# First norm's weights as the scale of the operations that split the turned tokens, with engine orders fixed around them

## The chip, the cores and the metric

The kernel runs on one core of one Trainium2 chip. The metric is the device time of one execution in microseconds. The engines are named as the profile names them: PE (TensorE, its weight loads as PEld), DVE (VectorE), ACT (ScalarE), POOL (GpSimd) and SP (SyncE, which issues the DMAs). A number such as L265 is a line of the kernel.

## The reference

One block of a streaming encoder: 16 learned meta tokens are put ahead of 512 tokens of width 1024. Two branches read one normalised input, a stick-breaking attention (8 heads) and a gated linear attention (GLA, 4 heads); they are merged by sigmoid gates, and a gated feed-forward stage with a causal convolution follows. The change touches the first norm and the first projections:

```python
h = jnp.concatenate([meta, x], axis=1)          # 528 tokens x 1024
hn = _rmsnorm(h, norm_mix_pre[l])               # x * rsqrt(mean(x^2) + eps) * g
proj = hn @ w_in[l]                             # all projections of both branches
g_q, g_k, g_v, g_r, g_lr = ...                  # slices of proj
glog = log_sigmoid(g_lr @ w_gk_up[l] + b_gk[l]) / 16
...
```

## The kernel before

Activations are held by feature: 128 features on the partitions, tokens along the free dimension, eight feature groups `k`. Every product has float32 accuracy by splitting both factors into a rounded high piece and a low remainder; a projection is three products for each `k` (high by high, low x by high w, high x by low w). A weight is loaded raw by SP, cast by ACT to its high piece (L90) and subtracted to its low piece (L91) on DVE or POOL.

The start of the program, with which the change deals, goes like this. Four token tiles of 128 (`xt1` to `xt4`) and the meta tokens (`xm`, as 128 rows of 128) are loaded with tokens on the partitions. For each, ACT sums the squares (L247) and a short chain of one-column operations gives 1/rms (L120 to L132); DVE scales the identity with it (L213, `drin`, two buffers). PE multiplies the tile by that diagonal (L265, `tp`): this turns it to features on the partitions and applies 1/rms in one. A 128 by 128 float32 product is two passes on PE, so a turn of one tile is 16 passes, in two PSUM tiles of 512 columns (four pieces `k` each). `split_g` then multiplies by the norm's weights (DVE, L206, `yg`, 128x512), casts the high piece (ACT, L207, `hnh`) and subtracts the low one (DVE or POOL, L208, `hnl`). The norm's weights `gT` come from an 8x128 load that PE turns (L234). Warming products (L230), whose result nobody reads, stand ahead of the first turn (10 of them) and behind turn 0, that of the meta tokens (6).

The first projections are k and q of GLA head 0 (L111, `pt_gk`, `pt_gq`), each in two halves of tokens: columns 0 to 271 (meta tokens, tiles 1 and 2) and 272 to 527 (tiles 3 and 4). With them come the gate's rank product (L383, `lr`), its copies (`gst`, L384 to L387), the gate products (L390, `pg`) with the weights `wg` (L372, L373), and then the v projections (`pt_gv`). Eight transposes of small tables (L305, L308: convolution weights, other norms' weights, the last two meta tokens) stand among the rank products; six DMAs load what they turn.

The order on each engine is made by a scheduler that places instructions by its own estimate of their times; `tc.issue_after(i)` pins what is built under it behind instruction `i`. A tile pool with `bufs=2` makes the third tile of a tag wait for the readers of the first. An instruction waits for others only through counters, one for each engine and DMA queue.

Of the kernel before, what the change touches and what calls it, by code (L numbers as in the profile page):

```python
# [16 lines left out]
P = 128  # L17
D = 1024
# [33 lines left out]
def block_kernel(ctx: ExitStack, tc: tile.TileContext, x, meta_tokens, norm_mix_pre, w_in, w_gk_up, b_gk,  # L52
# [26 lines left out]
    last_raw = [None]  # L79

    def load_w(src, nk, name, hi_out=None, lo_out=None, lo_eng=pool, into=None):
# [8 lines left out]
        act.copy(hi_out, raw)  # L90
        lo_eng.tensor_tensor(out=lo_out, in0=raw, in1=f32(hi_out), op=ALU.subtract)  # L91
        return hi_out, lo_out
# [7 lines left out]
    def proj(w, xh, xl, segs, name, apart=False):  # L100
# [4 lines left out]
        pt = mmt(f"pt_{name}")  # L105
        segs = [(pt[:m, 512 - l1 + l0 : 512], l0, l1), (pt[:m, 512 : 512 + l2 - l1], l1, l2)]
        steps = [(k, a, b) for k in range(nk) for a, b in ((wh, xh), (wh, xl), (wl, xh))]
        for grp in ([[s] for s in segs] if apart else [segs]):
            for n, (k, a, b) in enumerate(steps):
                for dst, lo, hi in grp:  # L110
                    pe.matmul(dst, a[:, k, :], b[:, k, lo:hi], start=n == 0, stop=n == len(steps) - 1)  # L111
        return pt[:m, 512 - l1 + l0 : 512 + l2 - l1]
# [56 lines left out]
    tables(SET_LN_EXP)  # L169
    ident = cst.tile([P, P], F32, name="ident")  # L170
    make_identity(nc, ident)
    p00 = ExitStack()
    p0c = p00.enter_context(tc.tile_pool(name="p0c", bufs=1, side="right"))
# [3 lines left out]
    tmpc = p0c.tile([P, P], F32, name="tmpc")  # L177
    pool.memset(tmpc, -1.0)
    pool.tensor_copy(neg1, tmpc)

    pool.affine_select(out=tmpc, in_=tmpc, compare_op=ALU.is_ge, fill=0.0, base=0, pattern=[[-1, P]], channel_multiplier=1)
    pool.tensor_copy(tri, tmpc)
    pool.memset(ucum, 1.0 / 16.0)
    pool.affine_select(out=ucum, in_=ucum, compare_op=ALU.is_ge, fill=0.0, base=0, pattern=[[1, P]], channel_multiplier=-1)

    ghT = cst.tile([P, 2], F32, name="ghT")
    cw = cst.tile([P, 4, FT], F32, name="cw")
# [21 lines left out]

    def diagonal(pl, r, n, nm):  # L210

        d = pl.tile([P, P], F32, tag="dr", name=f"dr{nm}", bufs=2)
        dve.tensor_scalar(out=d[:n, :n], in0=ident[:n, :n], scalar1=r, scalar2=None, op0=ALU.mult)  # L213
        return d[:n, :n]

    with tc.tile_pool(name="p0", bufs=2, side="right") as p0:
# [3 lines left out]
        g8 = p0.tile([KT, P], F32, name="g8", bufs=1)  # L220
        for i in (1, 2):
            sp.dma_start(xts[i], x[(i - 1) * P : i * P, :])
        sp.dma_start(g8, norm_mix_pre[0].rearrange("(k p) -> k p", p=P))
        sp.dma_start(xm, meta_tokens.rearrange("t (k p) -> (t k) p", p=P))

        def warm(n, nm):

            tp = pst(f"warm{nm}", "z")
            for _ in range(n):
                pe.matmul(tp[:, :P], ident, ident, start=True, stop=True)  # L230
# [11 lines left out]
        def stats(i, after=None):  # L242
            xt = xts.get(i, xm)
            junk = p0.tile([P, D], F32, tag="junk", name=f"junk{i}", bufs=1)
            ss = p0.tile([P, 1], F32, tag="ss", name=f"ss{i}")
            with tc.issue_after(after.ins) if after else ExitStack():
                act.activation(junk[:, : xt.shape[1]], xt, AF.Square, accum_out=ss)  # L247
            if not i:
                tp = pst("ssm")
                pe.matmul(tp[:, :1], same, ss, start=True, stop=True)  # L250
                ss = tp[:, :1]
            return diagonal(p0, rstd_of(p0, ss, D, f"in{i}"), P, f"in{i}")

        def turned(i, dr):
            if not i:
                tp = pst("tpm")
                last_tp[0] = pe.matmul(tp[:, :P], xm, dr, start=True, stop=True)
                split_g(p0, hnh[:, :, :NM], hnl[:, :, :NM], tp[:, :P].rearrange("p (t k) -> p k t", k=KT), gT, "m")
                return
            t = slice(NM + (i - 1) * P, NM + i * P)  # L260
            for b in range(2):
                tp = pst(f"tp{i}_{b}", "sz"[i % 2])
                for k in range(4):
                    c = (4 * b + k) * P
                    last_tp[0] = pe.matmul(tp[:, k * P : (k + 1) * P], xts[i][:, c : c + P], dr, start=True, stop=True)  # L265
                ks = slice(4 * b, 4 * b + 4)
                low = split_g(p0, hnh[:, ks, t], hnl[:, ks, t], tp.rearrange("p (k t) -> p k t", k=4), gT[:, ks], f"{i}_{b}", LO[i][b])
            return low

        last_tp = [None]  # L270
        LO = {1: (pool, pool), 2: (dve, pool), 3: (dve, pool), 4: (dve, pool)}
        d1 = stats(1)
        d2 = stats(2, last_exp[0])
        turned(1, d1)
        d0 = stats(0, last_exp[0])
        low2 = turned(2, d2)
        with tc.issue_after(last_exp[0].ins), tc.issue_after(last_yg[0].ins):
# [15 lines left out]
        cr = p0.tile([FT, 4, P], F32, name="cr", bufs=1)  # L293
        sp.dma_start(cr[:, 0:3, :], conv_w.rearrange("r (m p) -> m r p", p=P))
        sp.dma_start(cr[:, 3, :], conv_b[0].rearrange("(m p) -> m p", p=P))
        small = []
        for t, src in ((ghT, gla_head_norm[0]), (g1T, norm_mix_post[0]), (g2T, norm_ffn_pre[0]), (mT, meta_tokens[T0:, :])):
            n = src.shape[0] // P if len(src.shape) == 1 else src.shape[0] * KT
            r = p0.tile([n, P], F32, name=f"small{len(small)}", bufs=1)
            sp.dma_start(r, src.rearrange("(k p) -> k p" if len(src.shape) == 1 else "t (k p) -> (t k) p", p=P))  # L300
            small.append((t, r, n))
        with tc.issue_after(last_tp[0].ins):
            tp = pst("cwt")
            for r in range(4):
                pe.transpose(tp[:, r * FT : (r + 1) * FT], cr[:, r, :], ident[:FT, :FT])  # L305
            o = 4 * FT
            for t, r, n in small:
                pe.transpose(tp[:, o : o + n], r, ident[:n, :n])  # L308
                o += n
        act.copy(cw, tp[:, : 4 * FT].rearrange("p (r m) -> p r m", r=4))  # L310
        o = 4 * FT
        for t, r, n in small:
            src = tp[:, o : o + n]
            dve.tensor_copy(t, src.rearrange("p (t k) -> p t k", k=KT) if t is mT else src)
            o += n

    p00.close()
# [859 lines left out]
```

## Time and profile before

| | us |
|---|---|
| median of 3 runs | 955.11 (954.68 to 955.27) |
| profiled execution | 956.72 |
| its span, first to last instruction | 954.8 |

The mean granted clock of the span is 0.990. A row of the timeline gives start, length, engine, line, operation, output and inputs, form, count, and in brackets the idle time ahead of it with what ended it. A row of the chain gives start, length and what it was. Rows with x16 or x32 join neighbours of one kind; a matmul's own length overlaps the next one's, so its pace is read from starts. Times in the text are from the span's start.

### The profile page before, as it was taken

The page shows a single profiled execution, that of the slowest core. Times are in us where ns is not written, and L with a number is a line of the kernel's source. Part 1 is how long each engine was busy: PE and PEld are TensorE (multiplying, and loading weights), DVE is VectorE, ACT ScalarE, POOL GpSimd, SP SyncE. Part 2 cuts the span into 40 slices and gives each one's busy share as a digit, 9 for nine tenths or more (in the row PEclk, how much of TensorE's full clock was granted, in tenths as well). Part 3 has the DMA queues.
Part 4 walks back from the last instruction along what each step waited for, and adds up shares of the span by engine and source line. Part 5 has one row for each costly group of instructions (what it writes and reads, how often), then busy time and mean ns, then how long its engine had stood idle before and what let it go on. Part 6 is the DMA issues. An engine that isn't in the chain of part 4 may idle for free.

```text
span 954.8 us, 17806 instructions
## 1 busy us (share of the span) xinstructions
PE 926.2 (97%) x7164; PEld 854.3 (89%) x7164; DVE 655.4 (69%) x1110; ACT 492.3 (52%) x933; POOL 360.7 (38%) x262
## 2 busy tenths in 40 slices
PE   7999999999999998999999899999999999999996
PEld 7999999999999997999998679999999999988785
DVE  5676858687558785888849957554555444578987
ACT  5664656555467674676663245433333333255654
POOL 5433242333355444554445443544444444100200
PEclk9999999999999999999999999999999999999999
DMA  7122222212223212231214453333333333274923
GB/s 209 55 68 67 69 67 67 68 50 78 63 60 87 65 49 66 67 90 47 77 56 113 145 184 111 90 89 99 100 89 89 90 104 93 90 253 159 254 94 121
DMA packets 129731, 92.85 MB, mean 97 GB/s; under 512 B 4064, under 2 KB 114914, under 8 KB 129650
## 3 DMA queue, kind: packets, MB, share of 16 engines
q1 hardware_dynamic: 126178, 82.55, 29.4%
q0 software_dynamic: 1504, 2.88, 1.8%
q10 hardware_dynamic: 1968, 6.29, 1.8%
q8 instruction: 56, 0.92, 0.4%
q14 instruction: 25, 0.20, 0.1%
HBM read 87.52 MB, written 4.19 MB: 96 GB/s over the span
## 4 chain that ended last, share of the span: by engine, by line
PE 82%; DVE 10%; issue 3%; ACT 3%; POOL 2%; DMA 1%; DVEq 0%; ACTq 0%; POOLq 0%
PE pt_up L111 13%; PE ga L963 13%; PE pt_gv L111 5%; PE pt_gr L111 5%; PE pt_go L111 4%; PE pt_mg L111 4%; PE dA L1025 3%; PE dD L1025 3%; PE pt_gk L111 3%; PE pt_sv L111 2%; PE pt_gq L111 2%; PE dB L1025 2%; PE pt_ms L111 2%; PE wo L897 2%; PE pt_sk L111 2%
## 5 line engine op out<-in xcount | busy, mean ns | idle before, releaser
L91 POOL TENSOR_TENSOR wl_up<-raw_up,wh_up 128x1024 fp32r<-128x1024 f32 x22 | 53.0, 2410 | 67.9 <-ACT wh_up L90 67.9
L91 POOL TENSOR_TENSOR wl_ga<-raw_ga,wh_ga 128x1024 fp32r<-128x1024 f32 x22 | 55.2, 2510 | 56.6 <-ACT wh_ga L90 56.6
L111 PE MATMUL pt_up<-h2l,wh_up 128*128 128x256 f32 (+1 forms) x352 | 73.7, 283 | 0.5 <-POOL h2l L208 0.2
L111 PE MATMUL pt_up<-h2h,wh_up 128*128 128x256 f32 (+1 forms) x352 | 73.6, 283 | 0.2
L111 PE MATMUL pt_up<-h2h,wl_up 128*128 128x256 f32 (+1 forms) x352 | 73.2, 282 | 0.0
L963 PE MATMUL ga<-h2l,wh_ga 128*128 128x512 f32 (+1 forms) x192 | 72.2, 376 | 0.0
L963 PE MATMUL ga<-h2h,wl_ga 128*128 128x512 f32 (+1 forms) x192 | 72.2, 376 | 0.0
L963 PE MATMUL ga<-h2h,wh_ga 128*128 128x512 f32 (+1 forms) x192 | 72.0, 375 | 0.0
L90 ACT CAST wh_up<-raw_up 128x1024 fp32r<-128x1024 f32 x22 | 23.0, 1049 | 85.3 <-PE pt_up L111 76.2
L111 PEld LDWEIGHTS pt_up<-h2h,wh_up 128*128 128x128 f32 x352 | 56.9, 189 | 2.2 <-ACT h2h L207 0.5
L111 PEld LDWEIGHTS pt_up<-h2l,wh_up 128*128 128x128 f32 x352 | 55.5, 189 | 1.1 <-DVE h2l L208 0.7
L111 PEld LDWEIGHTS pt_up<-h2h,wl_up 128*128 128x128 f32 x352 | 55.4, 189 | 0.0
L963 PEld LDWEIGHTS ga<-h2h,wl_ga 128*128 128x128 f32 x192 | 36.2, 189 | 7.0
L954 DVE SCALAR_TENSOR_TENSOR cy<-pt_up,cw,cy 128x511 f32<-128x511 f32 (+1 forms) x22 | 16.4, 745 | 37.7 <-ACT cy L951 37.7
L963 PEld LDWEIGHTS ga<-h2l,wh_ga 128*128 128x128 f32 x192 | 36.1, 188 | 6.2
L963 PEld LDWEIGHTS ga<-h2h,wh_ga 128*128 128x128 f32 x192 | 36.2, 188 | 6.1
L954 DVE SCALAR_TENSOR_TENSOR yp<-pt_up,cw,yp 128x511 f32<-128x511 f32 (+1 forms) x22 | 16.4, 745 | 30.9 <-ACT yp L951 30.9
L90 ACT CAST wh_ga<-raw_ga 128x1024 fp32r<-128x1024 f32 x22 | 23.0, 1048 | 25.2 <-PE ga L963 24.7
L1053 POOL DMA_DIRECT2D tv<-in_w_ffn_down_dram x6 | 7.1, 1178 | 68.0 <-DVE wl_p L139 68.0
L91 POOL TENSOR_TENSOR wl_gr<-raw_gr,wh_gr 128x1024 fp32r<-128x1024 f32 x8 | 19.1, 2386 | 36.0 <-ACT wh_gr L90 27.1
L138 ACT CAST sh_p<-As 128x512 fp32r<-128x512 f32 (+1 forms) x30 | 17.4, 584 | 28.9 <-PE dB L1025 12.1
L111 PE MATMUL pt_gr<-hnh,wh_gr 128*128 128x258 f32 (+1 forms) x128 | 28.2, 294 | 0.0
(555 smaller groups left out, 3222.6 us busy)
## 6 DMA issues: line engine op xcount, KB each, us to landing
raw_up<-in_w_ffn_up_dram SPq DMA_DIRECT2D x22, 512.0 KB, 3.8
raw_ga<-in_w_ffn_gate_dram SPq DMA_DIRECT2D x22, 512.0 KB, 3.9
raw_t<-in_w_ffn_down_dram SPq DMA_DIRECT2D x10, 512.0 KB, 7.5
raw_gv<-in_w_in_dram SPq DMA_DIRECT2D x8, 512.0 KB, 3.8
raw_gr<-in_w_in_dram SPq DMA_DIRECT2D x8, 512.0 KB, 3.9
raw_mg<-in_w_in_dram SPq DMA_DIRECT2D x8, 512.0 KB, 3.9
raw_go<-in_w_gla_out_dram SPq DMA_DIRECT2D x8, 512.0 KB, 4.2
raw_ms<-in_w_in_dram SPq DMA_DIRECT2D x8, 512.0 KB, 3.9
```

The costliest lines, as they stand in the source:

```text
L90: act.copy(hi_out, raw)
L91: lo_eng.tensor_tensor(out=lo_out, in0=raw, in1=f32(hi_out), op=ALU.subtract)
L111: pe.matmul(dst, a[:, k, :], b[:, k, lo:hi], start=n == 0, stop=n == len(steps) - 1)
L138: act.copy(hi, src)
L897: pe.matmul(d0[i], m[k][:, t], w, start=k == 0 and q == 0, stop=k == 7 and q == 2)
L954: dve.scalar_tensor_tensor(out=y[:, d:], in0=pt[:, : SEQ - d], scalar=c, in1=y[:, d:], op0=ALU.mult, op1=ALU.add)
L963: pe.matmul(pg_[:, lo:hi], a[:, k, :], b[:, k, lo:hi], start=lo == 0 and k == 0 and q == 0, stop=k == KT - 1 and q == 2, skip_group_check= ...
L1025: mm[i] = pe.matmul(dsts[i], a, b, start=first and k == 0 and j == 0, stop=last and k == NP - 1 and j == 2, skip_group_check=True)
L1053: return lambda n, q, nk: pool.dma_start(out=t[:, q : q + nk, :], in_=block(s, c, q, nk), accum_op=ALU.add)
```

## The change

A new input `by_feature` (128x130, float32) holds the first norm's weights, three other small tables, two meta tokens and the convolution weights and biases, already with features on the partitions; the host only reshapes and joins them. One DMA loads it, and the transposes, their copies and their loads go. For the token tiles, `split_g` is replaced by operations on pieces of 128 columns that read PSUM directly: ACT writes the high piece as `tp` times `gT`, DVE writes the low piece as `tp` times `gT` minus the high piece. `split_g` stays for the meta tokens. The meta tokens' squares go to DVE, and their diagonal is made before that of tile 2. Three warming products stand ahead of turn 1, none behind turn 0. The low piece of q's weights moves from POOL to DVE. Tiles 3 and 4 are turned after the first halves of both k and q, and POOL builds masks and triangles later.

```diff
+        sp.dma_start(xts[1], x[0:P, :])
         sp.dma_start(xm, meta_tokens.rearrange("t (k p) -> (t k) p", p=P))
+        sp.dma_start(xts[2], x[P : 2 * P, :])
+        sp.dma_start(bf, by_feature)
...
         warm(10, 0)
-        tp = pst("g")
-        pe.transpose(tp[:, :KT], g8, ident[:KT, :KT])
-        act.copy(gT, tp[:, :KT])
...
+                sqm = p0.tile([P, P], F32, name="sqm", bufs=1)
+                dve.tensor_tensor(out=sqm, in0=xm, in1=xm, op=ALU.mult)
+                dve.tensor_reduce(out=ss, in_=sqm, op=ALU.add, axis=mybir.AxisListType.X)
...
-                ks = slice(4 * b, 4 * b + 4)
-                low = split_g(p0, hnh[:, ks, t], hnl[:, ks, t], tp.rearrange("p (k t) -> p k t", k=4), gT[:, ks], f"{i}_{b}", LO[i][b])
+                for k in range(4 * b, 4 * b + 4):
+                    c = slice((k - 4 * b) * P, (k - 4 * b + 1) * P)
+                    with tc.issue_after(last_hi[0].ins) if last_hi[0] else ExitStack():
+                        last_hi[0] = act.mul(hnh[:, k, t], tp[:, c], gT[:, k : k + 1])
+                    with tc.issue_after(last_yg[0].ins) if last_yg[0] else ExitStack():
+                        last_yg[0] = dve.scalar_tensor_tensor(out=hnl[:, k, t], in0=tp[:, c], scalar=gT[:, k : k + 1],
+                                                              in1=f32(hnh[:, k, t]), op0=ALU.mult, op1=ALU.subtract)
...
         d1 = stats(1)
+        d0 = stats(0, last_exp[0])
+        with tc.issue_after(last_tp[0].ins):
+            warm(3, 1)
         d2 = stats(2, last_exp[0])
...
-            first["q"] = load_w(cols(w_in, C_GQ), KT, "gq0")
-        turned(3, d3)
-        low4 = turned(4, d4)
+            first["q"] = load_w(cols(w_in, C_GQ), KT, "gq0", lo_eng=dve)
...
+        begun = {nm: proj(first[nm], hnh, hnl, ALL, f"g{nm}0", apart=True, only=(0,)) for nm in "kq"}
+        with tc.issue_after(last_pr[0].ins):
+            turned(3, d3)
+            turned(4, d4)
...
-            for r in range(4):
-                pe.transpose(tp[:, r * FT : (r + 1) * FT], cr[:, r, :], ident[:FT, :FT])
...
-                w = first[nm] if h == 0 else load_w(cols(w_in, c0), KT, f"g{nm}{h}")
-                pt = proj(w, hnh, hnl, ALL, f"g{nm}{h}", apart=h == 0)
+                if h == 0:
+                    with tc.issue_after(after_lr[0].ins):
+                        pt = proj(first[nm], hnh, hnl, ALL, f"g{nm}{h}", apart=True, only=(1,), pt=begun[nm])
```

In the rows below, `tp_0` and `tp_1` are the two PSUM tiles of a turn, numbers at the end of a name count buffers, and brackets name the counters that an instruction waits for (an engine's, or a DMA queue's as DMAHW). First PE before, from the first instruction to the first product of k:

```order
L230 MATMUL warm_112<-ident 128x128 x9
L234 MATMUL g<-ident,g_107 128x8 [waits DMAHW2_49]
L265 MATMUL tp_0_156<-drin_141,xt_102 128x128 [waits DMAHW0_49,DVE_49]
L250 MATMUL ssm<-ss_175,same 128x1 [waits Activation_49,Pool_49]
L265 MATMUL tp_0_189<-drin_154,xt_103 128x128 [waits DMAHW1_49,DVE_49]
L257 MATMUL tpm<-drin_187,xm 128x128 [waits DMAHW3_49,DVE_49,PE_49]
L230 MATMUL warm_221<-ident 128x128 x6
L111 MATMUL pt_gk_483<-hnh,wh_gk_209 128x272 [waits Activation_49]
L111 MATMUL pt_gk_483<-hnl,wh_gk_209 128x272 [waits DVE_49,Pool_49]
L111 MATMUL pt_gk_483<-hnh,wl_gk_210 128x272
L111 MATMUL pt_gk_483<-hnh,wh_gk_209 128x272
L111 MATMUL pt_gk_483<-hnl,wh_gk_209 128x272
```

And the same stretch of PE in the changed kernel:

```order
L225 MATMUL warm_96<-ident 128x128 x9
L246 MATMUL ssm<-ss_124,same 128x1 [waits DVE_49,Pool_49]
L225 MATMUL warm_140<-ident 128x128 x3
L262 MATMUL tp_0_157<-drin_122,xt_86 128x128 [waits DMAHW0_49,DVE_49,PE_49]
L254 MATMUL tpm<-drin_138,xm 128x128 [waits DMAHW1_49,DVE_49]
L262 MATMUL tp_0_195<-drin_155,xt_87 128x128 [waits DMAHW2_49,DVE_49]
L262 MATMUL tp_1_208<-drin_155,xt_87 128x128 [waits DVE_49]
L115 MATMUL pt_gk_255<-hnh,wh_gk_185 128x272 [waits Activation_49]
L115 MATMUL pt_gk_255<-hnl,wh_gk_185 128x272 [waits DVE_49]
L115 MATMUL pt_gk_255<-hnh,wl_gk_186 128x272
L115 MATMUL pt_gk_255<-hnh,wh_gk_185 128x272 [waits Activation_49]
L115 MATMUL pt_gk_255<-hnl,wh_gk_185 128x272 [waits DVE_49]
```

The turn of the meta tokens moved ahead of tile 2's, warming products ahead of turn 1, and the products of k wait for ACT and DVE at each piece, not once.

On ACT before, from the first split to the casts of the second tile:

```order
L207 CAST hnh<-yg_0_161 128x4x128 [waits DVE_49]
L207 CAST hnh<-yg_1_170 128x4x128 [waits DVE_49]
L90 CAST wh_gk_209<-raw_gk_207 128x1024 [waits DMAHW4_49]
L247 ACTIVATE junk_228,ss_229<-xt_104 128x1024 [waits DMAHW5_49]
L207 CAST hnh<-yg_0_194 128x4x128 [waits DVE_49]
L207 CAST hnh<-yg_1_203 128x4x128 [waits DVE_49]
```

And in the changed kernel, up to the cast of q's weights:

```order
L266 ACTIVATE hnh<-tp_0_157,bf 128x128 [waits DMAHW3_49,PE_49]
L266 ACTIVATE hnh<-tp_0_157,bf 128x128 [waits DVE_49] x3
L266 ACTIVATE hnh<-tp_1_170,bf 128x128 [waits PE_49]
L266 ACTIVATE hnh<-tp_1_170,bf 128x128 [waits DVE_49] x3
L90 CAST wh_gk_185<-raw_gk_183 128x1024 [waits DMAHW4_49]
L198 CAST hnh<-ygm 128x8x16 [waits DVE_49]
L266 ACTIVATE hnh<-tp_0_195,bf 128x128 [waits PE_49]
L266 ACTIVATE hnh<-tp_0_195,bf 128x128 [waits DVE_49] x3
L90 CAST wh_gq_225<-raw_gq_223 128x1024 [waits DMAHW7_49]
```

Two casts a tile became eight multiplies, and six of the eight wait for DVE; the weights' casts stand behind a whole token tile.

DVE of the changed kernel in the same stretch:

```order
L206 TENSOR_SCALAR drin_155<-ident,a_in_152 128x128 [waits DVE_49,PE_49]
L268 SCALAR_TENSOR_TENSOR hnl<-tp_0_157,bf,hnh 128x128 [waits DMAHW3_49,Activation_49]
L268 SCALAR_TENSOR_TENSOR hnl<-tp_0_157,bf,hnh 128x128 [waits Activation_49] x3
L268 SCALAR_TENSOR_TENSOR hnl<-tp_1_170,bf,hnh 128x128 [waits Activation_49] x4
L197 TENSOR_TENSOR ygm<-tpm,bf 128x128 [waits PE_49]
L91 TENSOR_TENSOR wl_gk_186<-raw_gk_183,wh_gk_185 128x1024 [waits DMAHW4_49,Activation_49]
L268 SCALAR_TENSOR_TENSOR hnl<-tp_0_195,bf,hnh 128x128 [waits Activation_49] x4
L91 TENSOR_TENSOR wl_gq_226<-raw_gq_223,wh_gq_225 128x1024 [waits DMAHW7_49,Activation_49]
```

Each low piece waits for ACT; the diagonal of tile 2 (`drin_155`) now stands ahead of the lows of tile 1 and waits for PE, and the low piece of q's weights stands behind those of tile 2.

More of the change, by code (lines that the diff above doesn't have):

```diff
@@ L98, in wrows, with proj @@
         return w[k0 * P : (k0 + nk) * P, c0:c1].rearrange("(k p) m -> p k m", p=P)
-    def proj(w, xh, xl, segs, name, apart=False):
+    last_pr = [None]
+    def proj(w, xh, xl, segs, name, apart=False, only=None, pt=None):
         wh, wl = w
@@ L104, in proj @@
         (l0, l1), (_, l2) = segs
-        pt = mmt(f"pt_{name}")
+        begins = only and pt is None
+        pt = mmt(f"pt_{name}") if pt is None else pt
         segs = [(pt[:m, 512 - l1 + l0 : 512], l0, l1), (pt[:m, 512 : 512 + l2 - l1], l1, l2)]
         steps = [(k, a, b) for k in range(nk) for a, b in ((wh, xh), (wh, xl), (wl, xh))]
+        segs = [segs[i] for i in only] if only else segs
         for grp in ([[s] for s in segs] if apart else [segs]):
@@ L176, in block_kernel @@
     ucum = cst.tile([P, P], F32, name="ucum")
[L177 to L187, printed above, removed]
+    bf = cst.tile([P, sum(WIDTHS)], F32, name="bf")
+    gT, ghT, g1T, g2T, mT, cw = (bf[:, sum(WIDTHS[:i]) : sum(WIDTHS[: i + 1])] for i in range(len(WIDTHS)))
+    mT = mT.rearrange("p (t k) -> p t k", k=KT)
+    cw = cw.rearrange("p (r m) -> p r m", m=FT)
     p1 = ExitStack()
@@ L219, in block_kernel @@
         xm = p0.tile([P, P], F32, name="xm", bufs=1)
[L220 to L223, printed above, removed]
+        sp.dma_start(xts[1], x[0:P, :])
         sp.dma_start(xm, meta_tokens.rearrange("t (k p) -> (t k) p", p=P))
+        sp.dma_start(xts[2], x[P : 2 * P, :])
+        sp.dma_start(bf, by_feature)
+        tables(SET_LN_EXP)
+        last_tp = [None]
         def warm(n, nm):
@@ L229, in warm @@
             for _ in range(n):
[L230 removed]
+                last_tp[0] = pe.matmul(tp[:, :P], ident, ident, start=True, stop=True)
         warm(10, 0)
[L233 to L235 removed]
         same = p0.tile([P, P], F32, name="same", bufs=1)
@@ L242, in stats @@
         def stats(i, after=None):
-            xt = xts.get(i, xm)
-            junk = p0.tile([P, D], F32, tag="junk", name=f"junk{i}", bufs=1)
             ss = p0.tile([P, 1], F32, tag="ss", name=f"ss{i}")
-            with tc.issue_after(after.ins) if after else ExitStack():
[L247 to L252, printed above, removed]
+            if i:
+                junk = p0.tile([P, D], F32, tag="junk", name=f"junk{i}", bufs=1)
+                with tc.issue_after(after.ins) if after else ExitStack():
+                    act.activation(junk, xts[i], AF.Square, accum_out=ss)
+            else:
+                sqm = p0.tile([P, P], F32, name="sqm", bufs=1)
+                dve.tensor_tensor(out=sqm, in0=xm, in1=xm, op=ALU.mult)
+                dve.tensor_reduce(out=ss, in_=sqm, op=ALU.add, axis=mybir.AxisListType.X)
+                tp = pst("ssm")
+                with tc.issue_after(last_tp[0].ins):
+                    last_tp[0] = pe.matmul(tp[:, :1], same, ss, start=True, stop=True)
+                ss = tp[:, :1]
+            with tc.issue_after(after.ins) if after else ExitStack():
+                return diagonal(p0, rstd_of(p0, ss, D, f"in{i}"), P, f"in{i}")
         def turned(i, dr):
@@ new lines, in turned @@
+                for k in range(4 * b, 4 * b + 4):
+                    c = slice((k - 4 * b) * P, (k - 4 * b + 1) * P)
+                    with tc.issue_after(last_hi[0].ins) if last_hi[0] else ExitStack():
[3 more added lines that the diff above has]
+                                                              in1=f32(hnh[:, k, t]), op0=ALU.mult, op1=ALU.subtract)
@@ L296, in block_kernel @@
[L296 to L303, printed above, removed]
-            for r in range(4):
[L305 to L317, printed above, removed]
+        first_half = last_hi[0], last_yg[0]
+        with tc.issue_after(first_half[0].ins), tc.issue_after(first_half[1].ins):
+            first["q"] = load_w(cols(w_in, C_GQ), KT, "gq0", lo_eng=dve)
+            d3 = stats(3)
+            d4 = stats(4)
@@ new lines, in block_kernel @@
+        with tc.issue_after(wst_lo.ins):
+            tmpc = pgc.tile([P, P], F32, name="tmpc")
+            pool.memset(tmpc, -1.0)
+            pool.tensor_copy(neg1, tmpc)
+            pool.affine_select(out=tmpc, in_=tmpc, compare_op=ALU.is_ge, fill=0.0, base=0, pattern=[[-1, P]], channel_multiplier=1)
+            pool.tensor_copy(tri, tmpc)
+            pool.memset(ucum, 1.0 / 16.0)
+            pool.affine_select(out=ucum, in_=ucum, compare_op=ALU.is_ge, fill=0.0, base=0, pattern=[[1, P]], channel_multiplier=-1)
```

155 lines of the change are left out of this document (75 added, 80 removed).

## The prediction

> **What bounds the kernel now.** First the summary of busy time and the chain of work that ended last.
>
> ```profile
> PE 926.2 (97%) x7164; PEld 854.3 (89%) x7164; DVE 655.4 (69%) x1110; ACT 492.3 (52%) x933; POOL 360.7 (38%) x262
> ...
> PE 82%; DVE 10%; issue 3%; ACT 3%; POOL 2%; DMA 1%; DVEq 0%; ACTq 0%; POOLq 0%
> ```
>
> TensorE is busy for 97% of the span, and DMA holds only 1% of the chain. So nothing later in the program absorbs a delay: a microsecond that PE loses at the start is a microsecond at the end. The diff reaches only the first 45 us (and the order of a few rows near 570 us), so I read the busy time by stretches of the start, then the chain there.
>
> ```profile
> 0.00:13.00 13.00, 10.61 (x55) 10.29 (x55) 4.13 (x14) 7.10 (x17) 7.00 (x26) 1.00 0.86 256
> 13.00:25.00 12.00, 9.61 (x78) 9.08 (x77) 11.14 (x21) 7.21 (x17) 5.77 (x5) 1.00 0.65 158
> 25.00:40.00 15.00, 15.00 (x123) 14.26 (x122) 11.77 (x26) 10.06 (x20) 5.72 (x11) 1.00 0.01 2
> ```
>
> The columns are the length, then PE, PE's weight loads, DVE, ACT and POOL, the granted clock, DMA share and GB/s. From 25 us on PE has no gap at all; what can be won is the 4.8 us of gaps before that (13.0 − 10.61 and 12.0 − 9.61) and PE's own work. DVE is already 93% busy (11.14 of 12.00) in the second stretch, so an engine plan that gives DVE more serial work here is dangerous.
>
> ```profile
> 7.23 3.78 PE tp L265 x16
> ...
> 17.84 3.13 PE pt_gk L111 x23
> 20.97 3.57 PE tp L265 x32
> ...
> 27.30 0.36 PE cwt L305 x4
> 27.65 0.24 PE cwt L308 x4
> ...
> 30.39 1.77 PE lr L383 x15
> ...
> 36.64 0.70 PE pg L390 x3
> ...
> 38.98 11.88 PE pt_gv L111 x96
> ```
>
> These are the milestones (start, length): turn 1 at 7.23, the unbroken k products at 17.84, first half of k done at 20.97, the v products at 38.98. From 20.97 to 38.98 PE works without a pause, 18.0 us.
>
> **The change, part by part.** *The split.* Before, one DVE multiply reads a whole 512-column PSUM tile, and from then on ACT and DVE or POOL work from SBUF.
>
> ```profile
> 9.34 0.69 DVE L206 TENSOR_TENSOR yg<-tp,gT 128x512 f32<-128x512 f32 x1 [0.64 <-PE tp L265]
> 10.06 0.62 ACT L207 CAST hnh<-yg 128x512 fp32r<-128x512 f32 x1 [1.89 <-DVE yg L206]
> ...
> 15.73 0.28 DVE L206 TENSOR_TENSOR ygm<-tpm,gT 128x128 f32<-128x128 f32 x1
> ```
>
> After, both halves read PSUM, in eight pieces of 128 columns per token tile. In the engine rows shown with the change, three of four ACT multiplies of a PSUM tile wait for DVE alone (the count that each waits for is that of the low of the piece before), and each DVE low waits for the ACT multiply of its own piece. The two engines therefore take turns. The page has no such operation, so I build it from the nearest rows.
>
> ```profile
> 27.94 0.23 ACT L310 COPY cw<-cwt 128x88 f32<-128x88 f32 x1 [1.94 <-PE cwt L308]
> ...
> 45.77 0.59 ACT L410 COPY gv<-pt_gv 128x528 f32<-128x528 f32 x1
> ```
> ```profile
> L951 ACT ACTIVATE yp<-pt_up,cw x11: 772/772/777, 606.5 to 822.1; 128x512 f32<-128x512 f32 x11
> ```
> ```profile
> L552 DVE SCALAR_TENSOR_TENSOR S<-S,el,pu x12: 469/479/483, 79.6 to 230.7; 128x256 f32<-128x256 f32 x12
> ```
> ```profile
> 606.51 0.77 ACT L951 ACTIVATE yp<-pt_up,cw 128x512 f32<-128x512 f32 x1
> ```
> ```profile
> 607.32 0.75 DVE L954 SCALAR_TENSOR_TENSOR yp<-pt_up,cw,yp 128x511 f32<-128x511 f32 x1 [6.97 <-ACT yp L951]
> ```
>
> ACT from PSUM: 0.23 at 88 columns and 0.59 at 528 give 0.82 ns a column, so 0.26 at 128 and 0.58 at 512. The activation with two per-partition pointers took 0.77 at 512, so each pointer adds about 0.1: **0.36** for a high piece. DVE: 0.28 at 128 and 0.69 at 512 give 1.07 ns a column, so 0.42 at 256; the operation with a pointer took 0.48 there, 0.06 more: **0.34** for a low piece. Handovers: 606.51 + 0.77 to 607.32 is 0.04 (ACT to DVE), 9.34 + 0.69 to 10.06 is 0.03 (DVE to ACT). One pair is **0.77 us**, and from the first low to the last of a token tile are seven steps, 5.4, less some 0.5 at the change of PSUM tile, where ACT waits for PE alone and may run ahead: about 4.9. From below, without the pointers, a pair is 0.26 + 0.28 + 0.07 = 0.60; were the turns not forced, the slower engine alone would set it, 0.36.
>
> *Turn 1.* The meta tokens' statistics move to DVE, and their sum product and three of the warming products (each two passes) now stand ahead of turn 1.
>
> ```profile
> 1.82 4.64 PE L230 MATMUL warm<-ident 128*128 128x128 f32 x20 [1.82 <-POOL ident masks.py:199]
> 6.89 0.29 DVE L213 TENSOR_SCALAR drin<-ident,a_in 128x128 f32<-128x128 f32 x1
> ...
> 10.80 0.43 PE L250 MATMUL ssm<-ss,same 128*128 128x1 f32 x2
> 11.09 2.17 PE L265 MATMUL tp<-drin,xt 128*128 128x128 f32 x16
> 12.30 1.04 ACT L90 CAST wh_gk<-raw_gk 128x1024 fp32r<-128x1024 f32 x1
> ...
> 14.60 1.22 DVE L91 TENSOR_TENSOR wl_gk<-raw_gk,wh_gk 128x1024 fp32r<-128x1024 f32 x1
> ```
>
> Twenty passes at some 0.22 and the sum product (0.43) hold PE to 6.6, six more passes to 7.9, so turn 1 starts 0.7 later than 7.23. Before, the passes of turn 1 took 0.24 each and those of turn 2 0.14 (2.17/16); the step came after 4.4 us of an unbroken stream (7.23 to about 11.6). Now the stream is hardly broken from 1.82, so the step may come at 6.2, or as late as before; I take about 8, turn 1 done at 10.2 (bounds 1.0 earlier, 1.5 later). The diagonal of tile 2 waits for all of turn 1 (it reuses the buffer) and stands ahead of the lows on DVE: 10.5. Lows run from 10.85 to **15.75**, where before the halves of turn 1 came from bigger, overlapped operations. The weights' cast (1.04) follows the last high on ACT to 16.35, its low (1.22) ends at 17.6, and the lows of turn 2 start at **18.1, +0.3** on 17.84. The second PSUM tile of turn 2 waits for the multiply of the meta tokens, behind all lows of turn 1: PE idles about 4.4 us there, on nobody's path but its own.
>
> *First half of k.* Before, 24 products ran at their own pace:
>
> ```profile
> 18.16 0.29 PE L111 MATMUL pt_gk<-hnh,wh_gk 128*128 128x272 f32 x1
> ...
> 20.68 0.29 PE L111 MATMUL pt_gk<-hnh,wl_gk 128*128 128x272 f32 x1
> ```
>
> Twenty steps in 2.52 us, 0.126 each, 0.38 for the three of a piece. Now each three wait for their low, one per pair, so lows set the pace: last low at 23.0, k done at 23.25 against 20.97: **+2.3** in all.
>
> *First half of q.* Its high weights follow the last high (23.5); the low weights, once on POOL beside this, now stand on DVE behind the last low and the cast: 23.5 + 1.22 = 24.75. PE has two products to do before: **1.25 us of new wait**.
>
> *Work.* From there PE has: 24 products (3.0), 32 passes of turns 3 and 4 (3.57), 16 of the gate's rank product (1.77/15 = 0.12, so 2.0), 64 products of the second halves at 0.118 (7.55), 5 gate products (0.70/3 = 0.23, so 1.15): 17.3. The eight transposes of small tables (0.36 + 0.24 = 0.6) are gone: 18.0 to 17.4, **−0.6**. The one DMA in their place (67 KB) is fourth in SP's queue, behind two x tiles and the meta tokens (1.1 MB); at the 256 GB/s of the first stretch all that takes 4.6 us from 0.8, and the first high piece needs it only after 10: hidden, unless it lands 4 us later than that.
>
> *Second halves.* They need tiles 3 and 4 for each k. The high and low pieces of turn 3 can begin with its first PSUM tile, at 28.65; eight pairs and the first of turn 4 put the first full k at 34.2, while PE is ready at 33.3: **0.9**. Then eight products a k (0.94) outlast a pair (0.77), so PE sets the pace. Behind the lows on DVE stand the four operations that build the gate's weights:
>
> ```profile
> 25.90 2.59 DVE L372 CAST wg<-rwg 16x512 fp32r<-16x512 f32 x3
> ...
> 29.25 0.69 DVE L373 TENSOR_TENSOR wg<-rwg,wg 16x512 fp32r<-16x512 f32 x1
> ```
>
> Last lows near 40, then some 2.8 for the four: gate products at 42.9 while PE is ready at 41.75, **1.1**; and the second v tile's cast stands on ACT behind the last gate copies and the eviction of k, **0.9**. *Sum*: +2.3 + 1.25 + 0.9 + 1.1 + 0.9 − 0.6 = 5.9, and with some 0.3 of handovers at the four seams **+6.2**: v products at 45.1 against 38.98. What POOL no longer does is worth little of this: its weight low slowed a diagonal that PE did not wait for.
>
> ```profile
> 19.07 2.46 DVE L213 TENSOR_SCALAR drin<-ident,a_in 128x128 f32<-128x128 f32 x1
> 19.07 2.38 POOL L91 TENSOR_TENSOR wl_gq<-raw_gq,wh_gq 128x1024 fp32r<-128x1024 f32 x1 [2.13 <-ACT wh_gq L90]
> ```
>
> The moved mask building on POOL has until 60 us; the reordered rows near 570 us lie in a full PE, ±0.5. The profiled execution of 956.72 (span 954.8) would become 962.9 (span 961.0); the median of the runs, 955.11, becomes **961.3**.
>
> **The rivals.** *A, no turns.* If high and low of different pieces overlap, each engine goes by its own operation: 0.36 a piece. Fourteen steps lie on the path (seven each in turns 1 and 2), so 14 × 0.41 = 5.7 go: **955.6**, not slower by more than 0.2%. It decides from a step of 0.77 − 6.2/14 = 0.33. For it: before, ACT and DVE overlapped freely. Against it: the waits in the rows. The Trainium skill's page PSUM — Partial Sum Buffer, section PSUM bank collisions raise a hardware error, has two engines keep off one bank at a time, even when both read; that is why these waits stand, and it speaks against A. No run here shows such a collision.
>
> *B, lighter pieces.* At 0.60 a pair, 14 × 0.17 = 2.4 go: **958.9**.
>
> *C, the clock falls.* PE's idle stretch at 11 to 15 us and the broken k products may cost it its speed.
>
> ```profile
> 573.79 3.63 PE L860 MATMUL mini<-ones,acc 128*128 128x1 f32 x32
> 577.28 3.12 PE L850 MATMUL ht<-drffn,hb 128*128 128x128 f32 x16
> ...
> 590.46 1.95 PE L850 MATMUL ht<-drffn,hb 128*128 128x128 f32 x16
> ```
>
> After 3.6 us of one-column products the same 16 passes took 3.12, not 1.95. In the k half a slow three (0.75) still fits a pair; if q's 24 are slow too, +3: **964.3**. Against it: q's own stream is dense. The Trainium skill's TensorE: Matmul & The Clock Gate, section Part 1: The HAM clock gate (the "warmup" mystery), has full rate after a busy window of about 3.4 us and half after an idle one, in windows that run free of the kernel; the step after 4.4 us and the slow ht agree, and by it the drop hangs on where the window falls.
>
> **How the numbers follow.** Main forecast (959.6 to 963.0) 0.62; B (957.4 to 959.6) 0.15; C (963.0 to 965.3) 0.14; A (953.0 to 957.4) 0.09. The range leaves out A and the edge of C: 957.5 to 965.0. A measurement of this kernel tells about 0.2% (1.9 us) from no change, so A gives 0.06 of same and 0.03 of faster; the rest, 0.91, is slower.
>
> **What would show it.** In the changed trace: high pieces each released by the DVE low before, lows 0.77 apart; k's first half from about 18.1 to 23.2 with PE waiting for DVE's lows; a wait for q's low weights near 24.7; PE's stretch from 25 to 40 us no longer full; v products at 45.1, and from there the same distances as before. Lows 0.4 apart would make the prediction wrong (A); so would products that start much before the lows of their token tile, or a stall that I have put in the sum and that PE fills.

## The result and the profile after

| | before | after |
|---|---|---|
| median of the runs, us | 954.89 (4 runs, 953.85 to 955.27) | 962.97 (4 runs, 962.15 to 963.20) |
| profiled execution, us | 956.72 | 963.20 |
| its span, us | 954.8 | 961.3 |

The ratio is 1.0085 (95% interval 1.0067 to 1.0102): slower by 0.9%, 8.1 us by the medians and 6.5 us between the two profiled executions. The chain of the changed kernel, where before PE alone stood from 18 us on:

```profile
7.40 2.04 PE tp L262 x16
10.04 0.38 ACT hnh L266
10.44 0.36 DVE hnl L268
10.83 0.38 ACT hnh L266
11.23 0.36 DVE hnl L268
...
21.48 0.37 ACT hnh L266
21.85 0.94 ACT wh_gq L90
22.82 1.24 DVE wl_gq L91
24.09 3.04 PE pt_gq L115 x22
...
45.97 11.46 PE pt_gv L115 x92
```

From 10 to 24 us the path runs through ACT and DVE by turns, and PE only joins it with q. The v products end at 45.97 + 11.46 = 57.43, before at 38.98 + 11.88 = 50.86: 6.6 us later, as much as the spans differ by. Behind them the two profiles gain and lose: the seam near 580 us took 1.6 us longer in the changed kernel (last section), the stretches ahead of it and behind it 1.7 us less together. The windows say the same of the engines (length, PE, weight loads, DVE, ACT, POOL, granted clock, DMA share, GB/s):

```profile
0.00:13.00 13.00, 8.66 (x54) 8.12 (x54) 4.65 (x20) 6.89 (x17) 2.91 (x12) 1.00 0.88 263
13.00:25.00 12.00, 8.82 (x41) 6.95 (x42) 6.60 (x16) 7.74 (x18) 0.00 (x0) 0.86 0.41 107
25.00:40.00 15.00, 13.91 (x113) 13.01 (x113) 7.75 (x25) 7.52 (x25) 2.95 (x13) 1.00 0.13 36
40.00:60.00 20.00, 18.69 (x169) 16.76 (x168) 12.68 (x27) 15.68 (x28) 11.25 (x16) 1.00 0.30 80
```

DVE's busy time from 13 to 25 us fell from 11.14 to 6.60 and its share is now 55%, and yet the stage is longer: an engine that takes turns with another is half idle, and its low share hides that it is the bound. PE lost its full stretch (13.91 of 15.00, and 18.69 of 20.00). On ACT and DVE the timeline shows the turns one by one:

```profile
10.04 0.37 ACT L266 ACTIVATE hnh<-tp,bf 128x128 fp32r<-128x128 f32 x1 [1.11 <-DVE hnl L268]
10.83 0.37 ACT L266 ACTIVATE hnh<-tp,bf 128x128 fp32r<-128x128 f32 x1 [0.42 <-DVE hnl L268]
11.61 0.63 ACT L266 ACTIVATE hnh<-tp,bf 128x128 fp32r<-128x128 f32 x2 [0.42 <-DVE hnl L268]
```
```profile
10.44 0.35 DVE L268 SCALAR_TENSOR_TENSOR hnl<-tp,bf,hnh 128x128 fp32r<-128x128 f32 x1 [0.43 <-ACT hnh L266]
11.23 0.35 DVE L268 SCALAR_TENSOR_TENSOR hnl<-tp,bf,hnh 128x128 fp32r<-128x128 f32 x1 [0.44 <-ACT hnh L266]
```

A high piece takes 0.37, a low piece 0.35, and each waits 0.42 to 0.44 for the other: a step of 0.79 us. Only at the change of PSUM tile do two highs follow each other (the x2 row).

PE's waits of the first 46 us, grouped (us in all, times, longest):

```profile
PE tp L262 <- DVE ygm L197: 4.3, 1, 4.3
...
PE pt_gq L115 <- DVE wl_gq L91: 0.7, 1, 0.7
PE pt_gv L115 <- ACT gq L401: 0.7, 1, 0.7
PE lr L346 <- DVE hnl L268: 0.6, 1, 0.6
...
PE pg L354 <- DVE wg L334: 0.5, 1, 0.5
```

### The profile page after: what moved, and what is told of

Its sections match the earlier page's. It is cut to its first block, busy times and chain, and to the rows that moved or that the text cites. A ratio compares the mean times of both kernels' runs of the same rounds, so it can differ in the third digit from the quotient of the medians.

```text
span 961.3 us, 17805 instructions
## 1 busy us (share of the span) xinstructions
PE 928.7 (97%) x7149; PEld 854.2 (89%) x7149; DVE 657.1 (68%) x1130; ACT 497.7 (52%) x953; POOL 351.8 (37%) x256
## 4 chain that ended last, share of the span: by engine, by line
PE 81%; DVE 11%; ACT 3%; issue 2%; POOL 1%; DMA 0%; DVEq 0%; POOLq 0%; ACTq 0%
PE pt_up L115 13%; PE ga L959 13%; PE pt_gr L115 5%; PE pt_gv L115 5%; PE pt_mg L115 4%; PE pt_go L115 4%; PE dA L1021 3%; PE dD L1021 3%; PE pt_sv L115 2%; PE dB L1021 2%; PE pt_gq L115 2%; PE pt_ms L115 2%; PE pt_gk L115 2%; PE wo L893 2%; PE pt_sk L115 2%
## 5 line engine op out<-in xcount | busy, mean ns | idle before, releaser
L950 DVE SCALAR_TENSOR_TENSOR cy<-pt_up,bf,cy 128x511 f32<-128x511 f32 (+1 forms) x22 | 16.4, 746 | 37.7 <-ACT cy L947 37.7
L950 DVE SCALAR_TENSOR_TENSOR yp<-pt_up,bf,yp 128x511 f32<-128x511 f32 (+1 forms) x22 | 16.4, 746 | 31.2 <-ACT yp L947 31.2
L91 POOL TENSOR_TENSOR wl_gr<-raw_gr,wh_gr 128x1024 fp32r<-128x1024 f32 x8 | 19.1, 2388 | 38.1 <-ACT wh_gr L90 38.1
L142 ACT CAST sh_p<-As 128x512 fp32r<-128x512 f32 (+1 forms) x30 | 17.4, 583 | 29.1 <-PE dB L1021 12.8
L115 PE MATMUL pt_gv<-hnh,wh_gv 128*128 128x272 f32 (+1 forms) x128 | 27.6, 290 | 0.8 <-ACT gq L401 0.7
```

The costliest lines, as they stand in the source:

```text
L91: last_wl[0] = lo_eng.tensor_tensor(out=lo_out, in0=raw, in1=f32(hi_out), op=ALU.subtract)
L115: last_pr[0] = pe.matmul(dst, a[:, k, :], b[:, k, lo:hi], start=n == 0, stop=n == len(steps) - 1)
L142: act.copy(hi, src)
L950: dve.scalar_tensor_tensor(out=y[:, d:], in0=pt[:, : SEQ - d], scalar=c, in1=y[:, d:], op0=ALU.mult, op1=ALU.add)
```

## The experiments

Theory 1: the cost is the forced turns of ACT and DVE inside a PSUM tile. Rival 2: it is the fixed orders around the split. Rival 3: it is PE's clock, which falls in the waits. Ratios are to the kernel before on the same chip.

| run | median, us | ratio | 95% interval |
|---|---|---|---|
| e_block: four highs, then four lows | 951.09 | 0.9954 | 0.9940 to 0.9968 |
| e_banks: pieces alternate between two PSUM tiles | 954.99 | 1.0002 | 0.9993 to 1.0011 |
| e_split: old split, new orders | 957.25 | 1.0026 | 1.0015 to 1.0036 |
| e_warm: PE kept busy in its gap | 964.50 | 1.0099 | 1.0085 to 1.0114 |
| e_part: old orders, pieces by turns | 964.59 | 1.0100 | 1.0075 to 1.0124 |
| e_bpart: old orders, four highs, then four lows | 954.88 | 1.0006 | 0.9992 to 1.0020 |
| e_half: twice the turns | 981.03 | 1.0271 | 1.0247 to 1.0296 |
| e_nowarm: e_block without three warming products | 952.30 | 0.9979 | 0.9965 to 0.9993 |

**The turns alone.** e_block issues the same 16 operations of a token tile; only their order inside a PSUM tile differs.

```diff
                 for k in range(4 * b, 4 * b + 4):
                     c = slice((k - 4 * b) * P, (k - 4 * b + 1) * P)
                     with tc.issue_after(last_hi[0].ins) if last_hi[0] else ExitStack():
                         last_hi[0] = act.mul(hnh[:, k, t], tp[:, c], gT[:, k : k + 1])
+                for k in range(4 * b, 4 * b + 4):
+                    c = slice((k - 4 * b) * P, (k - 4 * b + 1) * P)
                     with tc.issue_after(last_yg[0].ins) if last_yg[0] else ExitStack():
                         last_yg[0] = dve.scalar_tensor_tensor(out=hnl[:, k, t], in0=tp[:, c], scalar=gT[:, k : k + 1],
...
```

> The changed kernel with one edit: the four high pieces of a PSUM tile come first, then its four low pieces. The same 16 operations a token tile in the same engines' order, but ACT and DVE no longer take turns inside a PSUM tile, so that three of four waits go. Theory 1 (the forced turns are the cost): highs about 0.27 us apart and lows too, a token tile in about 3.4 us in place of 6.2, first half of k done near 16.6 in place of 22.6, no wait of the rank products for turn 3, v products near 35 in place of 46, time 950 to 953, below the kernel before. Rival 2 (the fixed orders are the cost: diagonal of tile 2 ahead of the lows, q's low weights on DVE, tiles 3 and 4 turned late): the gain stays under 2 us, 961 to 963. Rival 3 (PE's clock falls in its waits): 2 to 4 us of gain, in products that run at 0.13 in place of 0.23 us, with the waits for DVE still there.

951.09, inside the forecast of theory 1, against 962.97: the order of the eight operations on each PSUM tile was worth 11.9 us by the medians (11.5 by the profiled spans). DVE of this kernel, timeline rows:

```profile
10.34 2.16 DVE L270 SCALAR_TENSOR_TENSOR hnl<-tp,bf,hnh 128x128 fp32r<-128x128 f32 x8 [0.17 <-ACT hnh L266]
12.41 0.28 DVE L197 TENSOR_TENSOR ygm<-tpm,bf 128x128 f32<-128x128 f32 x1
12.61 1.21 DVE L91 TENSOR_TENSOR wl_gk<-raw_gk,wh_gk 128x1024 fp32r<-128x1024 f32 x1
13.74 0.28 DVE L199 TENSOR_TENSOR hnl<-ygm,hnh 128x128 fp32r<-128x128 f32 x1
14.10 2.16 DVE L270 SCALAR_TENSOR_TENSOR hnl<-tp,bf,hnh 128x128 fp32r<-128x128 f32 x8
```

Eight lows now take 2.16 us without a wait, 0.27 each: back to back, a piece is also cheaper than the 0.35 it takes alone. The chain of this kernel shows that PE has its full stretch again, from 14.5 us on:

```profile
14.51 2.53 PE pt_gk L115 x18
...
35.38 11.20 PE pt_gv L115 x92
```

The v products end at 46.58, 10.9 us ahead of the changed kernel and 4.3 ahead of the kernel before. By its median this is the fastest of all the versions. Rivals 2 and 3 gave at most 4 us; they fall as main causes.

**The distance between the turns.** In e_banks almost every high still waits for a low, but for the low of two pieces back, since neighbours lie in two PSUM tiles. The products of k and q take the pieces in the same order.

```diff
+ORDER = (0, 4, 1, 5, 2, 6, 3, 7)
...
+            for k in ORDER:
+                tp = tps[k // 4]
+                c = slice((k % 4) * P, (k % 4 + 1) * P)
...
-        steps = [(k, a, b) for k in range(nk) for a, b in ((wh, xh), (wh, xl), (wl, xh))]
+        steps = [(k, a, b) for k in (ORDER if only else range(nk)) for a, b in ((wh, xh), (wh, xl), (wl, xh))]
```

> The changed kernel with the pieces in the order 0 4 1 5 2 6 3 7, so that neighbours lie in two PSUM tiles, and the first and second halves of k and q taking their products in the same order. Every high piece still waits for a low, but for one two pieces back, in its own PSUM tile. Theory 1: a step of about 0.41 us (the longer operation and one handover) in place of 0.78, a token tile in 3.7 us, time 951 to 955. Rival 2: no change, 961 to 963. If the waits as such cost, whatever their distance: 961 to 963 too.

954.99, at the upper end of what theory 1 gave. ACT's rows:

```profile
10.36 0.63 ACT L270 ACTIVATE hnh<-tp,bf 128x128 fp32r<-128x128 f32 x2 [0.66 <-DVE hnl L272]
11.15 0.63 ACT L270 ACTIVATE hnh<-tp,bf 128x128 fp32r<-128x128 f32 x2 [0.16 <-DVE hnl L272]
11.93 0.63 ACT L270 ACTIVATE hnh<-tp,bf 128x128 fp32r<-128x128 f32 x2 [0.16 <-DVE hnl L272]
```

Two pieces a step of 0.79 us, 0.39 each: half the price, as expected of a pair of PSUM tiles. So a wait is not dear as such; a wait for the operation just issued is. The Trainium skill's page PSUM — Partial Sum Buffer, section PSUM bank collisions raise a hardware error, asks for a guard for each bank. The waits behave so here: pieces in one PSUM tile exclude each other, pieces in two overlap. What happens without the guard was not tried.

**The orders alone.** e_split puts the old split into the new orders.

```diff
+                ks = slice(4 * b, 4 * b + 4)
+                with tc.issue_after(last_hi[0].ins) if last_hi[0] else ExitStack(), tc.issue_after(last_yg[0].ins) if last_yg[0] else ExitStack():
+                    last_low[0] = split_g(p0, hnh[:, ks, t], hnl[:, ks, t], tp.rearrange("p (k t) -> p k t", k=4), gT[:, ks], f"{i}_{b}", LO[i][b])
```

> The changed kernel with the split of the kernel before put back: DVE multiplies 512 columns, ACT casts, DVE or POOL subtract from SBUF; the small tables' load, the warming products and all fixed orders stay. Theory 1: at least 5 of the 8 us come back, 952 to 956, k's first half done near 19. Rival 2: 960 to 963, since the orders are still there.

957.25, a miss by 1.25 us: 5.7 of the 8 us came back, and the rest did not. With the old split the new orders cost 2.1 us by the medians. The loss is not in the start of k, whose products begin at 17.19, ahead of the 17.84 of the kernel before. The trace shows longer waits of PE, and a fall of its clock in them. For the first wait:

```profile
12.79 2.08 DVE L91 TENSOR_TENSOR wl_gk<-raw_gk,wh_gk 128x1024 fp32r<-128x1024 f32 x1 [1.44 <-ACT wh_gk L90]
...
14.99 1.27 DVE L197 TENSOR_TENSOR yg<-tp,bf 128x512 f32<-128x512 f32 x2
...
16.38 0.53 PE L115 MATMUL pt_gk<-hnh,wh_gk 128*128 128x272 f32 x1 [3.81 <-ACT hnh L198]
```
```profile
11.29 2.50 POOL L199 TENSOR_TENSOR hnl<-yg,hnh 128x512 fp32r<-128x512 f32 x2 [7.68 <-ACT hnh L198]
```

The low piece of k's weights takes 2.08 beside POOL's lows of turn 1, against 1.21 in e_block. It now stands ahead of turn 2's multiplies on DVE, which start at 14.99 (12.40 before), and PE waits 3.8 us for their highs. The second wait is 2.2 us (30.5 to 32.6), for a low of turn 4 that stands on DVE behind the casts of the gate's weights. Behind both waits PE is slow, as the chain shows:

```profile
17.19 2.95 PE pt_gk L115 x12
...
20.39 1.39 PE pt_gk L115 x11
...
35.35 2.19 PE pt_gk L115 x12
```

The granted clock is 0.50 from 17.1 to 19.8 us and 0.57 from 33.6 to 37.5. At the pace of the row at 20.39 (0.126 a product) the two rows of 12 would take 3.0 us together in place of 5.1, so by this estimate the clock alone costs some 2 us here. So rival 2 holds for a smaller part, and only with the old split: the orders make the waits, and part of the price is rival 3's. How the two share it was not tested. In this profile the v products end at 54.87, 4.0 us later than before.

**The pieces in the old orders.** e_part and e_bpart are the kernel before with `split_g` replaced, by turns and in fours. Both are the loop above, here with the tables and all orders of before:

```diff
-                low = split_g(p0, hnh[:, ks, t], hnl[:, ks, t], tp.rearrange("p (k t) -> p k t", k=4), gT[:, ks], f"{i}_{b}", LO[i][b])
+                for k in range(4 * b, 4 * b + 4):
+                    c = slice((k - 4 * b) * P, (k - 4 * b + 1) * P)
...
+                        last_hi[0] = act.mul(hnh[:, k, t], tp[:, c], gT[:, k : k + 1])
...
+                        low = last_yg[0] = dve.scalar_tensor_tensor(out=hnl[:, k, t], in0=tp[:, c], scalar=gT[:, k : k + 1],
```

> The kernel before with one edit, the pieces that take turns in place of its split; the rest, the orders too, as the scheduler then places it. Theory 1 (the forced turns are the cost): 13 pairs of 0.78 us between the cast of k's weights and the first product of k, which starts near 26 in place of 17.8, less the turns of tiles 3 and 4 that PE does meanwhile: 960 to 964. Rival 2 (the fixed orders are the cost): within 1.5 us of the kernel before, 954 to 957.

> The kernel before with one edit, the pieces in its place of the split, four highs and then four lows of a PSUM tile. Theory 1: no turns inside a PSUM tile, so the pieces help by themselves: no lows on POOL, lows 0.27 us apart, the unbroken k products from about 15.5 in place of 17.8, 952 to 954. Rival 2: 955 to 957, the gain of the blocked pieces comes only with the fixed orders.

By turns: 964.59 beside 954.06 of the kernel before, measured together, just above the forecast of theory 1. The turns cost about 10 us in the old orders as well; they need no change of order to be dear. The wait stands elsewhere than forecast: PE waits 9.3 us in one piece for a low, ahead of the meta tokens' turn, and k's products but the first start at 30.6, not near 26, behind all the turns. A part of the 10 us is the clock's: behind that wait 16 passes take 2.98 us on the chain (granted clock 0.50 from 24 to 28 us), and the next 16 take 1.78. In fours: 954.88, no difference from before, so the second forecast missed by 0.9 us: there k's products start at 19.1, not 15.5. ACT of e_bpart shows one reason:

```profile
13.43 1.06 ACT L90 CAST wh_gk<-raw_gk 128x1024 fp32r<-128x1024 f32 x1
14.37 1.08 ACT L247 ACTIVATE junk<-xt 128x1024 f32<-128x1024 f32 x1
15.32 0.21 ACT L247 ACTIVATION_READ_ACCUMULATOR junk<-xt 128x1 f32 x1
15.42 1.15 ACT L269 ACTIVATE hnh<-tp,gT 128x128 fp32r<-128x128 f32 x4
```

The cast of k's weights and the squares of tile 3, which nobody needs yet, stand ahead of turn 2's last four highs, and on DVE the low piece of k's weights stands behind their lows (17.73 to 18.86 on the chain). Turn 1 is another: its 16 passes take 3.8 us, as in the kernel before, and 1.95 in e_block. The blocked pieces paid only with the new orders: fours in old orders 0, fours in new orders 4 us faster, the old split in new orders 2 us slower. Which of the new orders does it was not separated.

**Twice the turns.** e_half cuts each piece into two of 64 tokens.

```diff
+                    for h in (0, 64):
+                        ch, th = slice(c.start + h, c.start + h + 64), slice(t.start + h, t.start + h + 64)
...
+                            last_hi[0] = act.mul(hnh[:, k, th], tp[:, ch], gT[:, k : k + 1])
```

> The changed kernel with each piece cut in two halves of 64 tokens, high and low of each half taking turns: twice the turns for the same data. A turn of half a piece is estimated at 0.32 (ACT) + 0.28 (DVE) + 0.07 = 0.66 us from the 128-column rows, a token tile at 10.6 in place of 6.2 us. Theory 1: 4.4 us more for each of turns 1 and 2, about 4 for turn 3 and 3 for turn 4, which now outlasts PE: 974 to 980. Rival 2 or 3: under 3 us more, 963 to 966.

981.03, 1 us above the range. DVE's rows:

```profile
10.42 0.28 DVE L270 SCALAR_TENSOR_TENSOR hnl<-tp,bf,hnh 128x64 fp32r<-128x64 f32 x1 [0.38 <-ACT hnh L268]
11.09 0.28 DVE L270 SCALAR_TENSOR_TENSOR hnl<-tp,bf,hnh 128x64 fp32r<-128x64 f32 x1 [0.38 <-ACT hnh L268]
```

0.67 a step, as estimated. Half the data in a step costs 85% of the whole step: what is paid is mostly the fixed part of two operations and two handovers. Not all of the 18 us are steps, though: PE's granted clock is 0.55 from 13 to 25 us here, and the q products behind the wait for their low weights, which no low paces, run slow on the chain:

```profile
33.33 5.18 PE pt_gq L115 x22
```

In the changed kernel the same row takes 3.04.

**The clock and the warming products.** e_warm fills PE's gap in turn 2:

```diff
+                if i == 2 and b:
+                    wt = mmt("warmgap")
+                    with tc.issue_after(last_tp[0].ins):
+                        for _ in range(16):
+                            last_tp[0] = pe.matmul(wt[:, :P], ident, ident, start=True, stop=True)
```

> The changed kernel with 16 more warming products in PE's gap between the two PSUM tiles of turn 2 (10.9 to 15.2 us). Theory 1: the passes at 15.2 and the first products of k run at full rate again (0.11 and 0.13 us in place of 0.21 and 0.23), but the lows set the pace, so the first half of k still ends at 22.6 and the time stays within 0.4 us of 963.0. Rival 3: the time falls by 1.5 us or more.

964.50, which is 1.5 us above the changed kernel and so outside the 0.4 that theory 1 allowed; the intervals of the two overlap, and the profiled spans are 961.6 and 961.3. No gain, so rival 3 falls for this kernel. PE in windows (length, busy, clock, DMA share, GB/s), first the changed kernel, then e_warm:

```profile
11.00:15.00 4.00, 0.00 (x0) 1.00 1.05 236
15.00:19.30 4.30, 3.89 (x17) 0.60 0.56 153
19.30:23.00 3.70, 3.67 (x18) 1.00 0.19 58
```
```profile
11.00:15.00 4.00, 3.48 (x32) 1.00 1.00 214
15.00:19.30 4.30, 3.32 (x18) 1.00 0.56 150
19.30:23.00 3.70, 3.70 (x17) 0.58 0.19 56
```

The clock did fall after the idle stretch (0.60), and the warming products did prevent that, but with the k products still spaced by the lows it fell one window later (0.58). In both cases the slow stretch lies inside the wait for the lows and costs nothing: the first half of k is done at 22.84 and 22.86. Where no low paces PE behind a wait, the fall does cost, as in e_split and e_half. The Trainium skill's page TensorE: Matmul & The Clock Gate, section Part 1: The HAM clock gate (the "warmup" mystery), gives half rate after an idle window of about 3.4 us; the first of the two agrees with that. The second came without a pause as long as that, in broken work, and in e_split the clock fell behind a wait of 2.2 us. The prediction took the slow `ht` passes of the kernel before as agreement too; there PE was not idle but busy with one-column products, so that row shows a fall behind light work. How little work is enough for a fall, no run here shows.

e_nowarm takes the `warm(3, 1)` ahead of turn 1 out of e_block.

> The blocked kernel (four highs, then four lows) without the three warming products ahead of turn 1. By the term of the prediction that priced them (they delay turn 1 by up to 0.7 us) it gains 0.2 to 0.7 us, 950.4 to 950.9. By the other reading (they keep PE's stream unbroken, so that the clock steps up before turn 1) turn 1 runs at 0.22 to 0.24 us a pass again, ends 1 to 1.5 us later, and so does everything behind it: 952 to 953.

952.30, in the range of the second reading, but the profile shows another thing: there turn 1 starts at 7.15, runs at full pace (16 passes in 2.05 us) and this execution, at 950.61, is the fastest of its twelve runs (950.61 to 955.88). The intervals of e_block and e_nowarm overlap a little. Whether the three products help in some executions stays open; between these two profiles turn 1 starts 0.2 us earlier without them (7.15 for 7.38), not the 0.7 of the prediction. They are not what lets turn 1 run at full pace: its 16 passes took 3.78 us in the three profiles with the old orders (before, e_part, e_bpart) and 1.95 to 2.05 in all seven with the new ones, e_nowarm among them. The first warming product starts at 1.81 or 1.82 in the old orders and at 1.53 in the new; whether that is the reason was not tested.

## Why the prediction was right, point by point

The forecast was 961.3 and 962.9 for a profiled execution; measured were 962.97 and 963.20. The mechanism is shown by e_block, e_part and e_half. The terms:

- *The pair*: priced at 0.36 + 0.34 + 0.07 = 0.77, measured 0.37 + 0.35 and 0.79 a step. The seven steps from the first low of turn 1 to its last took 4.97 by their starts (9.66 to 14.63), forecast 4.9.
- *Turn 1*: mis-sized, inside the bounds that the prediction gave it. It started at 7.40, not 7.9, and its 16 passes took 2.04 us, so the clock had stepped up before it: the lows ran from 9.66 to 14.98, where the forecast has 10.85 to 15.75. The lows of turn 2 began at 16.91, not 18.1, which is 0.9 us ahead of the k stream before, where the sum had +0.3. PE's idle stretch in turn 2 came as forecast (4.3 us, forecast 4.4) and cost nothing.
- *First half of k*: done at 22.8, forecast 23.25; +1.9 in place of +2.3. Behind the last low PE needed 0.6 us, not 0.25.
- *q's low weights*: the place was right, the wait 0.7, not 1.25: the low piece was ready at 24.04, and PE's two products ahead of it, which started at 22.84, did not end before 23.3.
- *Between q and the second halves*: the sum had 0.9 of wait ahead of the second halves; the wait stood elsewhere. The rank product waited 0.6 for turn 3's lows, since it takes over a PSUM buffer of that turn, which the prediction did not see, and the second halves began at 33.73 (34.2). Behind them the lows of turn 4 were held up by the three copies of the gate on ACT (33.59 to 34.74), which the prediction left out.
- *Gate and v*: gate products 42.57 (42.9), as forecast behind the gate's weights, with a wait of 0.5 in place of 1.1. The five took 1.95, not 1.15: their weight loads waited for DVE in between (`gst` 0.39, `X` 0.42). The last wait before v (0.7) was for q's eviction on ACT, behind the cast of the second v weights, the same queue and nearly the price (0.9).
- *The sum*: +6.2 forecast, 6.6 at the end of the v products. That it fits so well is partly luck. Waits of PE from q on come to 3.0 us (0.74, 0.61, 0.47, 0.48 and 0.69), where the sum has 4.15, and 0.3 for handovers. The work from 22.84 to the first v product at 44.52, without the first four of these waits, took 19.4 us, where the sum has 17.4; most of that is in the gate products (+0.8), the second halves with their rank products (8.1, not 7.55) and q (3.4, not 3.0). The sum took the pace of unbroken streams for streams that break, and priced the breaks too high.

Of the rivals, A (no turns) is what e_block and e_banks built by hand, with the price it named or better: 951.09 and 954.99 for a forecast of 955.6. The waits in the rows were the right reason against it. B (lighter pieces) fell with 0.79. C saw a real fall of the clock, in the place it named, but q's products ran at full pace, so its 3 us did not come; in e_half, where q's products did run slow, 2.1 came. The warning about a busy DVE pointed elsewhere: DVE had less to do than before, and its turns with ACT set the pace.

The medians differ by 1.5 us more than the profiled pair. Single executions of the kernel before range from 952.7 to 958.8 over the comparisons, and its profiled one lay 1.8 above its median. Part of that has a place: from the last row of `cum` products (198.70) to the first `mini` (573.79) this profile took 375.1 us, the longest of the ten (371.9 to 374.3 in the others). Why is open. So a stage's end tells more of a change to that stage than the span of one execution does.

## What to carry to other kernels

Where two engines read one PSUM tile, issue all of one engine's operations on it, then all of the other's: high by high, then low by low, the same 16 operations cost 12 us less here than by turns. Read the waits of every instruction behind the first in a loop: a wait for the operation just issued on another engine turns two engines into one, and busy shares fall while it happens. Look at PE's pace behind every long wait too: where nothing else paces it there, the fall of its clock adds to the price of the wait. A reordering is worth what the stage's bound allows: the fours gained 4 us in the new orders and nothing in the old ones.

## What the runs showed of the hardware

The clock fell a second time, at the seam before the feed-forward stage, in some of the profiled executions only. PE rows of the changed kernel and of e_banks at the same work:

```profile
579.87 4.58 PE L856 MATMUL mini<-ones,acc 128*128 128x1 f32 x32
584.32 3.76 PE L846 MATMUL ht<-drffn,hb 128*128 128x128 f32 x16
```
```profile
571.56 3.63 PE L860 MATMUL mini<-ones,acc 128*128 128x1 f32 x32
575.05 2.03 PE L850 MATMUL ht<-drffn,hb 128*128 128x128 f32 x16
```

The windows of the changed kernel from 582.5 to 589.5 have a granted clock of 0.53; those of e_banks there stay at 1.00:

```profile
582.50:589.50 7.00, 7.00 (x31) 0.53 0.48 139
```
```profile
574.30:580.00 5.70, 5.04 (x34) 1.00 0.37 103
```

In the kernel before it fell too, but only behind the 32 one-column products (they took 3.63 and the 16 passes 3.12). From the first of them to the sum of squares behind (`msmix`) it is 10.4 us in the changed kernel, 8.8 before and 7.9 in e_banks. So one and the same piece of work differs by 2.5 us between the profiles of the changed kernel and e_banks, as much as a small change is worth, at a place that e_banks does not touch.

The granted clock does not show every slow stretch. The windows of the kernel before read 1.00 up to 13 us, although the passes of turn 1 ran at 0.24 us each (3.78 for 16) and those of turns 3 and 4 at 0.11 (3.57 for 32). The first step of the clock can be seen in the pace alone.
